# V's weights in load order, gates on ScalarE's queue, a fourth raw buffer, and mixed chunks in a layer with a product-key expert sub-layer

## The chip, the cores and the metric

One core of one Trainium2 chip. The time is in device microseconds (us) for one execution of the whole program; lower is better.

## The reference

One layer: adaptive norms, a mixing sub-layer (pooling and differential attention, projections in and out), a gated residual, then a sub-layer of 16384 single-neuron experts chosen by product keys, another gated residual and a final norm. The part that matters here, for 512 latent tokens of width 2048:

```
q = h @ Wq                        # 8 heads x 2 halves of 128
s1, s2 = q_half @ keys            # 128 scores for each half
top 16 of each half, then the top 16 of the 16 x 16 sums; g = softmax of them
expert e = 128 * i1 + i2
y = sum over heads and picks of  g * gelu(h . U[e]) * V[e]
```

## The kernel before

The program is one stream of work, dealt to five in-order engines by a scheduler that fixes each engine's order at build time. The stages of interest, in us of the profiled execution: norms and transposes to about 1153, queries ("wq", 16 half-heads, L626) to 1350, the first 72 tiles of U (L745) to 2053, then U's other 56 tiles and all of V to 3600, and the end.

For the last 368 latent tokens the experts are computed densely: for each of 128 blocks of 128 experts, a "u tile" makes gelu(h . U) by 48 matmuls (two loads of 512 KB from `ut`), is multiplied by a matrix of gates (mostly zero) and split into `a_hi` and `a_lo`; then V's rows of the block are multiplied by it. For the other 144 tokens SLOTS of single rows of U and V are gathered by GpSimd (`row`, `f`, `acc` in the names), and VectorE makes a multiply-add of 128x2048 of each (L696, L708). `pump` spreads them over the u tiles and the V loads.

Every weight comes by `weights()`: SyncE issues a load of 512 KB into one of 3 `raw` buffers (L126), ScalarE casts it to `whi` (L119), VectorE makes the rest `wlo` (L120; a_hi and a_lo, and fq_hi and fq_lo, go over the same two lines), each with 3 buffers, and TensorE makes three matmuls for each pair of pieces: hi by hi, hi by lo, lo by hi. In V a load is two rows of 512 numbers for each of 128 partitions and gives 24 matmuls (L953).

The gates of the dense tokens are built beside the first 72 u tiles and stored to DRAM (`g_s`). As they are complete only at the end, those 72 tiles are stored unmultiplied to `sg_s` ("kept" below; "spilled" in the title of the change). The last stage goes over 16 chunks of CH = 8 blocks: first 7 chunks of the 56 "fresh" blocks, whose u tiles are made there, then 9 chunks of the 72 kept ones, which are read back. For each 4 blocks a tile of gates `gt` (736 KB) is loaded. The names `raw`, `sg` (3 buffers, for fresh and kept tiles alike), `gt` (2 buffers) and `a_hi`, `a_lo` (9 each) are pools' tiles: a load waits until the tile that had its buffer has been read.

```
for c in range(NC):
    for n, ib in enumerate(ibs):                   # 8 blocks
        if n % 4 == 0: gt = ...; load gt           # L931
        sg = u_tile(ib, ...) or load sg_s[ib]      # L745, or L936
        sg = sg * gt                               # L937, VectorE
        a_hi, a_lo = split(sg)
    for dq in range(4):                            # four quarters of the output's width
        for n in range(0, 8, 2): weights(V ...); 24 matmuls   # L953
        accT[...] += pv[i]                         # L964, VectorE, four of them
```

Before the wq stage two more large copies matter: `f_hi` and `f_lo` (2944 KB each, packets of 368 numbers) are copied out of `fq_hi` and `fq_lo` by SyncE (L582, L583), and `keys` (1024 KB) is loaded by ScalarE (L604).

Of the kernel before, what the change touches and what calls it, by code (L numbers as in the profile page):

```python
# [10 lines left out]
F32 = mybir.dt.float32  # L11
# [18 lines left out]
NKEY = 128  # L30
# [4 lines left out]
GB = 16  # L35
# [30 lines left out]
SPILL = 72  # L66
# [4 lines left out]
GEND = 2  # L71
GRATE = 1.25
SLOTS = 256 + 2 * GB
RATE = (SLOTS - (SPILL - PRE - GS) * GRATE) / (2 * NKEY - SPILL - 11)


def body(tc, xin, ctx, vecs, lamv, ada1, ada2, adab2, n2g, fing, win, poolw, wout, wq, keys,
         ut, u, v, rope, icnt, out):
    nc = tc.nc
    V, S, G, E = nc.vector, nc.scalar, nc.gpsimd, nc.tensor  # L80

    with ExitStack() as whole:
        def pool(stack, name, bufs=1, space=None, side=None):
            kw = {} if space is None else {"space": space}
            if side is not None:
                kw["side"] = side
            if space is not DRAM:
                kw["reuse_waits"] = "tile"
            return stack.enter_context(tc.tile_pool(name=name, bufs=bufs, **kw))
# [28 lines left out]
        def split(dst_hi, dst_lo, src):  # L118
            S.copy(dst_hi, src)  # L119
            V.tensor_sub(dst_lo, src, dst_hi.bitcast(F32))  # L120

        def weights(src, shape):
            raw = wp.tile(shape, F32, name="raw", bufs=3)
            hi = wp.tile(shape, F32R, name="whi", bufs=3)
            lo = wp.tile(shape, F32R, name="wlo", bufs=3)
            nc.sync.dma_start(raw, src)  # L126
            split(hi, lo, raw)
            return hi, lo
# [87 lines left out]
        for k in range(KT):  # L216
            for j, c0, bs in ((0, 260, slice(2, 6)), (1, 2, slice(0, 2))):
                n = bs.stop - bs.start
# [370 lines left out]


        ub = pool(whole, "ub")
        ustack = ExitStack()
        psU = pool(ustack, "psU", 1, PSUM)
        rtstack = ExitStack()
# [81 lines left out]


        acc0 = gp.tile([128, D], F32, name="acc0")
        vw = v.rearrange("(a b) d -> a b d", b=NKEY)

        rows = [gp.tile([128, D], F32, name=f"row{i}") for i in range(3)]

# [74 lines left out]
        with ExitStack() as st:  # L757
            gb = pool(st, "gb")
            ps = pool(st, "psG", 1, PSUM)
            picks = {}  # L760

            def pick(b):
                ia, ib = (gb.tile([128, 128], F32, name=n, bufs=1) for n in ("ia", "ib"))
                gt = gb.tile([128, 128], F32, name="gt", bufs=1) if b else gate0
                decode(b, ia, ib, gt)
                if b == 0:
                    V.scalar_tensor_tensor(ia, ia, float(NKEY), ib, op0=OP.mult, op1=OP.add)
                    V.tensor_copy(e0, ia)
                    return
                if b == 1:  # L770
                    ef = gb.tile([128, 128], F32, name="ef")
                    ei = gb.tile([128, 128], I32, name="ei")
                    V.scalar_tensor_tensor(ef, ia, float(NKEY), ib, op0=OP.mult, op1=OP.add)
                    V.tensor_copy(ei, ef)
                    for q in range(GQ):
                        ps_, cs = slice(q * GB, (q + 1) * GB), slice(q * GB, (q + 1) * GB)
                        nc.scalar.dma_start(eB[ps_, :], ei[0:GB, cs])
                        nc.scalar.dma_start(gateB[ps_, :], gt[0:GB, cs])
                pt = ps.tile([128, 3, 128], F32, name="pt", bufs=1)
                for i, x in enumerate((ia, ib, gt)):  # L780
                    E.transpose(pt[:, i, :], x, ident)
                picks[b] = gb.tile([128, 3, 128], F32, name="pT", bufs=3)
                S.copy(picks[b], pt)

            def combine():

                for g in range(NG):
                    ge = gb.tile([128, 128, TG], F32, name="ge", bufs=1)
                    for t4 in range(0, TG, 4):
                        m = min(4, TG - t4)  # L790
                        pg = ps.tile([128, 4, 128], F32, name="pg", bufs=2)
                        for i in range(m):
                            b, t = divmod(T - TD + g * TG + t4 + i, 128)
                            pT = picks[b]
                            L = gb.tile([128, 128], F32, name="L", bufs=6)
                            R = gb.tile([128, 128], F32, name="R", bufs=6)
                            V.tensor_scalar(L, iota, pT[:, 0, t:t + 1], None, op0=OP.is_equal)
                            V.tensor_scalar(R, iota, pT[:, 1, t:t + 1], pT[:, 2, t:t + 1], op0=OP.is_equal, op1=OP.mult)
                            E.matmul(pg[:, i, :], L, R, start=True, stop=True)  # L799
                        S.copy(ge[:, :, t4:t4 + m].rearrange("p b t -> p t b"), pg[:, 0:m, :])  # L800
                        if t4 + 4 < TG:
                            yield
                    nc.scalar.dma_start(g_s[g], ge)
                    yield

            def few_end_steps():

                sel = gb.tile([128, GB], F32, name="sel")
                V.tensor_copy(sel, ident[:, 0:GB])
                for q in range(1, GQ):  # L810
                    V.tensor_add(sel, sel, ident[:, q * GB:(q + 1) * GB])
                z = gb.tile([128, D], F32, name="zB")[0:GB, :]
                ss = gb.tile([128, 4], F32, name="ssB")[0:GB, :]
                rs = gb.tile([128, 1], F32, name="rsB")[0:GB, :]
                tmp = gb.tile([128, 1], F32, name="tmpB")[0:GB, :]
                for dq in range(4):
                    ds = slice(dq * 512, (dq + 1) * 512)
                    gx = gb.tile([128, 512], F32, name="gxB", bufs=2)[0:GB, :]
                    nc.scalar.dma_start(gx, m_s[:, 3 * D + dq * 512:3 * D + (dq + 1) * 512].to_broadcast([GB, 512]))
                    xc = gb.tile([128, 512], F32, name="xcB", bufs=2)[0:GB, :]  # L820
                    nc.scalar.dma_start(xc, x1_s[1][0:GB, ds])
                    pb = ps.tile([128, 512], F32, name="pt", bufs=1)[0:GB, :]
                    E.matmul(pb, sel, acc0[:, ds], start=True, stop=True)
                    V.tensor_mul(z[:, ds], pb, gx)
                    V.tensor_add(z[:, ds], z[:, ds], xc)
                    S.activation(gx, z[:, ds], AF.Square, accum_out=ss[:, dq:dq + 1])
                    yield 1
                V.reduce_sum(rs, ss, axis=AX.X)
                V.tensor_scalar(tmp, rs, 1.0 / D, EPS, op0=OP.mult, op1=OP.add)
                G.tensor_tensor(rs, tmp, nhalf[0:GB, 0:1], OP.pow)  # L830
                for dq in range(4):
                    ds = slice(dq * 512, (dq + 1) * 512)
                    fg = gb.tile([128, 512], F32, name="gxB", bufs=2)[0:GB, :]
                    nc.scalar.dma_start(fg, fing[:, ds].to_broadcast([GB, 512]))
                    V.scalar_tensor_tensor(z[:, ds], z[:, ds], rs, fg, op0=OP.mult, op1=OP.mult)
                    nc.scalar.dma_start(out[128:128 + GB, ds], z[:, ds])
                    yield 1

            few_end_of.append(few_end_steps)
            spill(PRE)  # L840
            pick(1)
            steps = combine()
            todo, made, late = SPILL - PRE, 0, dict(LATE)
            nsteps = NG * ((TG + 3) // 4)
            for n in range(todo):
                spill(1)
                if n in late:
                    pick(late[n])
                if n >= GS:
                    pump(GRATE)  # L850
                while made < nsteps * (n + 1) / (todo - GEND):
                    made += 1
                    next(steps, None)
            assert made >= nsteps
# [40 lines left out]
        with ExitStack() as st:  # L895
# [23 lines left out]
                    if dq < 3:  # L919
                        V.tensor_mul(z[b][0:n, ds], z[b][0:n, ds], fg[0:n, :])  # L920

            order = list(range(SPILL, NKEY)) + list(range(SPILL))
            NC = NKEY // CH
            for c in range(NC):
                ibs = order[c * CH:(c + 1) * CH]
# [2 lines left out]
                for n, ib in enumerate(ibs):  # L928
                    if n % 4 == 0:
                        gt = ab.tile([128, NG, 4 * TG], F32, name="gt", bufs=2)  # L930
                        nc.sync.dma_start(gt, g_s[:, :, ib:ib + 4, :].rearrange("a p b t -> p a (b t)"))  # L931
                    if ib >= SPILL:
                        sg = u_tile(ib, bank()[:, 0:TD])
                    else:
# [9 lines left out]
                for dq in range(4):  # L944
                    pv = [bank()[:, 0:TD] for _ in range(4)]
                    for n in range(0, CH, 2):
                        hi, lo = weights(vw[:, ibs[n]:ibs[n] + 2, dq * 512:(dq + 1) * 512], [128, 2, 512])
                        for j in range(2):
                            a_hi, a_lo = A[n + j]
                            for i in range(4):  # L950
# [42 lines left out]
def prep(x, c, ctx, c_ctx, ada_w, ada_b, norm1_g, w_in, pool_w, pool_b, pool_scale,  # L993
         diff_lambda, subln_g, w_out, norm2_g, peer_wq, peer_keys, peer_u, peer_v, final_g):
    A = {}
# [24 lines left out]
    A["ut"] = peer_u[0].reshape(128, 128, 16, 128).transpose(1, 3, 2, 0)  # L1020
    A["u"] = peer_u[0]
    A["v"] = peer_v[0]
    f = np.float32
    t = np.arange(512)
    inv = (f(10000.0) ** (-np.arange(16, dtype=f) / f(16))).astype(f)
# [22 lines left out]
```

## Time and profile before

| what | us |
|---|---|
| median of 3 runs (lowest, highest) | 3621.0 (3616.66, 3635.32) |
| the profiled execution | 3616.92 |
| its span in the trace | 3615.1 |
| TensorE matmuls (PE) busy | 3473.2 (96%) |
| VectorE (DVE) busy | 2714.1 (75%) |
| ScalarE (ACT) busy | 1382.8 (38%) |
| GpSimd (POOL) busy | 525.6 (15%) |

A row of a timeline gives the start and the duration of an instruction (xN: of N merged ones), its line and its tiles as out<-in, and in brackets how long its engine sat idle before it and what ended that. SPq and ACTq are the queues of SyncE and ScalarE in which DMAs are issued. PEclk is TensorE's granted clock as a share of 2.4 GHz.

### The profile page before, as it was taken

What the parts mean: (1) busy time and instruction counts of PE and PEld (TensorE: products, weight loads), DVE (VectorE), ACT (ScalarE), POOL (GpSimd) and SP (SyncE); (2) the same over time, 40 slices, a digit from 0 to 9 for tenths busy, and PEclk for the clock granted to TensorE, in tenths of its full rate; (3) what the DMA queues carried; (4) which work ended last, traced back from release to release, by engine and by line L of the source; (5) the groups of instructions that cost most, each with busy time, mean ns of one, the idle gap of its engine ahead of it and who ended that gap; (6) DMA issues with size and microseconds to landing.
All of it is one profiled execution on the core that took longest, in us unless ns stands there. A gap on an engine that the chain in (4) does not pass through costs nothing.

```text
span 3615.1 us, 52998 instructions
## 1 busy us (share of the span) xinstructions
PE 3473.2 (96%) x20499; PEld 3230.3 (89%) x20499; DVE 2714.1 (75%) x4450; ACT 1382.8 (38%) x1987; POOL 525.6 (15%) x423
## 2 busy tenths in 40 slices
PE   7999999999998999999999999999999999999998
PEld 2588888899886889998999999999999999999998
DVE  5787787755536999997778677677677778888775
ACT  7554545555323223443334333223223322233233
POOL 1000000000031001111111122122122122112100
PEclk9999999999999999999999999999999999999999
DMA  9755555522547325887888887787787888988975
GB/s 332 266 178 173 173 170 176 156 66 72 197 140 217 112 91 207 307 292 285 289 315 325 295 324 267 277 325 266 282 327 287 287 321 313 322 317 316 318 242 173
DMA packets 295399, 885.74 MB, mean 245 GB/s; under 512 B 27345, under 2 KB 83386, under 8 KB 255466
## 3 DMA queue, kind: packets, MB, share of 16 engines
q1 hardware_dynamic: 223354, 494.45, 40.7%
q0 software_dynamic: 45600, 316.73, 22.9%
q10 hardware_dynamic: 26192, 71.18, 5.9%
q8 instruction: 160, 2.62, 0.3%
q14 instruction: 93, 0.76, 0.1%
HBM read 819.09 MB, written 51.35 MB: 241 GB/s over the span
## 4 chain that ended last, share of the span: by engine, by line
PE 57%; issue 14%; DMA 12%; DVE 10%; POOL 4%; ACT 4%; ACTq 0%; SPq 0%; DVEq 0%; POOLq 0%
PE pv L953 15%; PE pu L745 11%; PE zl L275 6%; PE pv L745 5%; PE pq L626 5%; PE zc L275 4%; PE pw L547 4%; DMA aw<-in_ada_dram 4%; DMA raw<-in_v_dram 3%; POOL row L690 2%; DVE wlo L120 2%; PE pg L799 2%; DMA sg<-sg_s 2%; DMA g_s<-ge 2%; PE sc L363 1%
## 5 line engine op out<-in xcount | busy, mean ns | idle before, releaser
L119 ACT CAST whi<-raw 128x1024 fp32r<-128x1024 f32 x664 | 695.5, 1050 | 1439.2 <-PE pv L953 305.9
L120 DVE TENSOR_TENSOR wlo<-raw,whi 128x1024 fp32r<-128x1024 f32 x664 | 822.7, 1244 | 429.6 <-ACT whi L119 420.4
L953 PE MATMUL pv<-a_hi,wlo 128*128 128x368 f32 x2048 | 684.0, 334 | 27.0 <-DVE wlo L120 27.0
L953 PE MATMUL pv<-a_hi,whi 128*128 128x368 f32 x2048 | 681.7, 333 | 8.1 <-ACT whi L119 8.1
L953 PE MATMUL pv<-a_lo,whi 128*128 128x368 f32 x2048 | 681.0, 333 | 0.0
L953 PEld LDWEIGHTS pv<-a_hi,wlo 128*128 128x128 f32 x2048 | 389.0, 190 | 32.8 <-DVE wlo L120 32.8
L953 PEld LDWEIGHTS pv<-a_hi,whi 128*128 128x128 f32 x2048 | 388.8, 190 | 9.5 <-ACT whi L119 9.5
L745 PE MATMUL pu<-f_hi,whi 128*128 128x368 f32 x1152 | 389.8, 338 | 1.3 <-ACT whi L119 1.0
L953 PEld LDWEIGHTS pv<-a_lo,whi 128*128 128x128 f32 x2048 | 388.7, 190 | 0.0
L745 PE MATMUL pu<-f_hi,wlo 128*128 128x368 f32 x1152 | 383.8, 333 | 4.0 <-DVE wlo L120 4.0
L745 PE MATMUL pu<-f_lo,whi 128*128 128x368 f32 x1152 | 381.1, 331 | 0.0
L745 PE MATMUL pv<-f_hi,whi 128*128 128x368 f32 x896 | 296.1, 330 | 1.3 <-ACT whi L119 1.3
L745 PE MATMUL pv<-f_hi,wlo 128*128 128x368 f32 x896 | 295.9, 330 | 1.2 <-DVE wlo L120 1.2
L745 PE MATMUL pv<-f_lo,whi 128*128 128x368 f32 x896 | 293.9, 328 | 0.0
L708 DVE SCALAR_TENSOR_TENSOR acc<-row,w,acc 128x2048 f32<-128x2048 f32 x111 | 260.6, 2347 | 0.0
L696 DVE SCALAR_TENSOR_TENSOR row<-row,f 128x2048 f32<-128x2048 f32 x109 | 248.6, 2287 | 9.6 <-DMA row<-in_u_dram,e 9.6
L275 PE MATMUL zl<-h_hi,whi 128*128 128x512 f32 (+1 forms) x640 | 239.2, 374 | 0.0
L690 POOL DMA_INDIRECT row<-in_v_dram,e x96 | 154.7, 1612 | 529.8 <-DVE acc L708 496.5
L275 PE MATMUL zl<-h_lo,whi 128*128 128x512 f32 (+1 forms) x640 | 223.7, 349 | 0.0
L275 PE MATMUL zl<-h_hi,wlo 128*128 128x512 f32 (+1 forms) x640 | 223.6, 349 | 0.0
L745 PEld LDWEIGHTS pu<-f_hi,wlo 128*128 128x128 f32 x1152 | 218.8, 190 | 4.9 <-DVE wlo L120 4.9
L745 PEld LDWEIGHTS pu<-f_hi,whi 128*128 128x128 f32 x1152 | 219.0, 190 | 2.8 <-ACT whi L119 1.9
(275 smaller groups left out, 6524.7 us busy)
## 6 DMA issues: line engine op xcount, KB each, us to landing
raw<-in_ut_dram SPq DMA_DIRECT2D x256, 512.0 KB
raw<-in_v_dram SPq DMA_DIRECT2D x256, 512.0 KB
aw<-in_ada_dram SPq DMA_DIRECT2D x256, 256.0 KB
raw<-in_win_dram SPq DMA_DIRECT2D x80, 512.0 KB
aw<-in_ada_dram SPq DMA_DIRECT2D x64, 512.0 KB
g_s<-ge ACTq DMA_DIRECT2D x8, 2944.0 KB
gt<-g_s SPq DMA_DIRECT2D x32, 736.0 KB
raw<-in_wout_dram SPq DMA_DIRECT2D x40, 512.0 KB
```

Source lines behind the costliest of these rows:

```text
L119: S.copy(dst_hi, src)
L120: V.tensor_sub(dst_lo, src, dst_hi.bitcast(F32))
L275: E.matmul(part[0], x[:, k8, :], y[:, k, part[1]], start=k == 0 and p == 0, stop=k == KT - 1 and p == 2)
L363: E.matmul(sc[:, cs], x[:, m, qs], y[:, cs], start=p == 0, stop=p == 1)
L547: E.matmul(pw[b], x[:, k, bs], y[:, j, :], start=i + j == 0 and p == 0, stop=i + j == KT - 1 and p == 2)
L626: E.matmul(pq[:, cs], a[:, k8, :], b[:, k, cs], start=k == 0 and p == 0, stop=k == KT - 1 and p == 2)
L690: G.indirect_dma_start(out=row, out_offset=None, in_=table, in_offset=bass.IndirectOffsetOnAxis(ap=e[:, j:j + 1], axis=0))
L696: tc.keep_in_program_order(V.scalar_tensor_tensor(row, row, 1.0, f0, op0=OP.mult, op1=OP.mult, accum_out=s0[:, j:j + 1]))
L708: tc.keep_in_program_order(V.scalar_tensor_tensor(acc0, row, w0[:, j:j + 1], acc0, op0=OP.mult, op1=OP.add))
L745: E.matmul(pu, a[:, k8, :], b[:, k, :], start=k == 0 and p == 0, stop=k == KT - 1 and p == 2)
L799: E.matmul(pg[:, i, :], L, R, start=True, stop=True)
L953: E.matmul(pv[i], x[:, j, ks], y, start=n + j == 0 and p == 0, stop=n + j == CH - 1 and p == 2)
```

## The change

Four edits. V's weights are handed over as a second copy `vd` in which the 4096 bytes that a partition takes in one load lie together (before: two pieces of 2048). The gates `gt` are issued from ScalarE's queue. Every fourth load goes into a further buffer `raw_0` that lies in the pool `ub`, from the wq stage on; its place is won by one buffer instead of two for `gxB` and `xcB`. And 14 chunks are made of 4 fresh and 4 kept blocks each, followed by 2 chunks of kept ones.

```
+RAWS = 1
+        turn, more = [0], []
+        def raw_buffer(shape):
+            turn[0] = (turn[0] + 1) % (3 + len(more))
+            if turn[0] < 3:
+                return wp.tile(shape, F32, name="raw", bufs=3)
+            return more[turn[0] - 3](shape)
         def weights(src, shape):
-            raw = wp.tile(shape, F32, name="raw", bufs=3)
+            raw = raw_buffer(shape)
...
         ub = pool(whole, "ub")
+        more.extend([lambda shape, i=i: ub.tile(shape, F32, name=f"raw_{i}") for i in range(RAWS)])
...
-                    gx = gb.tile([128, 512], F32, name="gxB", bufs=2)[0:GB, :]
+                    gx = gb.tile([128, 512], F32, name="gxB", bufs=1)[0:GB, :]
...
-            order = list(range(SPILL, NKEY)) + list(range(SPILL))
+            fresh, kept = list(range(SPILL, NKEY)), list(range(SPILL))
+            order = []
+            while fresh:
+                order += fresh[:4] + kept[:4]
+                fresh, kept = fresh[4:], kept[4:]
+            order += kept
...
-                        nc.sync.dma_start(gt, g_s[:, :, ib:ib + 4, :].rearrange("a p b t -> p a (b t)"))
+                        nc.scalar.dma_start(gt, g_s[:, :, ib:ib + 4, :].rearrange("a p b t -> p a (b t)"))
...
-                        hi, lo = weights(vw[:, ibs[n]:ibs[n] + 2, dq * 512:(dq + 1) * 512], [128, 2, 512])
+                        hi, lo = weights(vd[ibs[n] // 2, dq], [128, 2, 512])
...
+    A["vd"] = peer_v[0].reshape(128, 64, 2, 4, 512).transpose(1, 3, 0, 2, 4)
```

What this does to the engines' orders, at three places. **SyncE, start of the wq stage.** The names with `wq` are the loads of the half-heads, two for each; 11020 is the first load of the second half-head. Before:

```order
L126 DMA raw_11020<-in_wq_dram 128x1024
L126 DMA raw_11050<-in_wq_dram 128x1024
L126 DMA raw_11146<-in_wq_dram 128x1024
L126 DMA raw_11176<-in_wq_dram 128x1024
L582 DMA f_hi_10685<-fq_hi_10690 128x16x368
L583 DMA f_lo_10686<-fq_lo_10691 128x16x368
L126 DMA raw_11240<-in_wq_dram 128x1024
```

After:

```order
L136 DMA raw_11050<-in_wq_dram 128x1024
L136 DMA raw_11146<-in_wq_dram 128x1024
L136 DMA raw_11176<-in_wq_dram 128x1024
L592 DMA f_hi_10685<-fq_hi_10690 128x16x368
L593 DMA f_lo_10686<-fq_lo_10691 128x16x368
L136 DMA raw_0_11020<-in_wq_dram 128x1024
L136 DMA raw_0_11240<-in_wq_dram 128x1024
```

The load of 11020 now has the buffer `raw_0`, and stands behind the copies of f_hi and f_lo instead of ahead of the loads 11050 to 11176. It waits for the last of the tiles that lay in that place (the residual's rows, which the transposes and the copies of f to f0 read).

**SyncE, the passage from the u tiles to the V loads of a chunk.** Before, in the fifth of the fresh chunks, from the first load of V on:

```order
L126 DMA raw_24760<-in_v_dram 128x2x512
L126 DMA raw_24790<-in_v_dram 128x2x512
L126 DMA raw_24822<-in_v_dram 128x2x512
L126 DMA raw_24854<-in_v_dram 128x2x512
L126 DMA raw_24892<-in_v_dram 128x2x512
L126 DMA raw_24924<-in_v_dram 128x2x512
L931 DMA gt_25570<-g_s_79 128x8x184
L126 DMA raw_24954<-in_v_dram 128x2x512
```

After, in the seventh chunk, from the third load of V on (`sg` are the loads of the four kept tiles, called A4 to A7 below; the fresh ones are A0 to A3, and the loads of V v0 to v15, of which this row is v2):

```order
L136 DMA raw_0_25244<-in_vd_dram 128x1024
L136 DMA raw_25274<-in_vd_dram 128x1024
L136 DMA raw_25314<-in_vd_dram 128x1024
L136 DMA raw_25346<-in_vd_dram 128x1024
L952 DMA sg_25150<-sg_s_78 128x368
L952 DMA sg_25157<-sg_s_78 128x368
L136 DMA raw_0_25376<-in_vd_dram 128x1024
L952 DMA sg_25164<-sg_s_78 128x368
L952 DMA sg_25171<-sg_s_78 128x368
```

The gates have left this queue. Four loads of kept tiles stand between those of V: A4 and A5 behind v5, A6 and A7 behind v6.

**VectorE, the same passage.** Before, in the fifth chunk, from wlo of v3 on:

```order
L120 TENSOR_TENSOR wlo_24856<-raw_24854,whi_24855 128x1024
L708 SCALAR_TENSOR_TENSOR acc0_12695<-row2_12698,w0_13343,acc0_12695 128x2048
L120 TENSOR_TENSOR wlo_24894<-raw_24892,whi_24893 128x1024
L708 SCALAR_TENSOR_TENSOR acc0_12695<-f0_9445,w0_13343,acc0_12695 128x2048
L120 TENSOR_TENSOR wlo_24926<-raw_24924,whi_24925 128x1024
L708 SCALAR_TENSOR_TENSOR acc0_12695<-row0_12696,w0_13343,acc0_12695 128x2048
L964 TENSOR_TENSOR accT_19774<-accT_19774,pv_24756 128x368
L964 TENSOR_TENSOR accT_19774<-accT_19774,pv_24757 128x368
L964 TENSOR_TENSOR accT_19774<-accT_19774,pv_24758 128x368
L964 TENSOR_TENSOR accT_19774<-accT_19774,pv_24759 128x368
L120 TENSOR_TENSOR wlo_24956<-raw_24954,whi_24955 128x1024
```

After, in the seventh chunk, from the third gathered row behind the last u tile on:

```order
L718 SCALAR_TENSOR_TENSOR acc0_12695<-f0_9445,w0_13343,acc0_12695 128x2048
L121 TENSOR_TENSOR a_lo_25161<-sg_25157,a_hi_25160 128x368
L121 TENSOR_TENSOR a_lo_25168<-sg_25164,a_hi_25167 128x368
L953 TENSOR_TENSOR sg_25171<-sg_25171,gt_25148 128x368
L121 TENSOR_TENSOR wlo_25276<-raw_25274,whi_25275 128x1024
L121 TENSOR_TENSOR a_lo_25175<-sg_25171,a_hi_25174 128x368
L718 SCALAR_TENSOR_TENSOR acc0_12695<-row0_12696,w0_13343,acc0_12695 128x2048
L980 TENSOR_TENSOR accT_19774<-accT_19774,pv_25178 128x368
L980 TENSOR_TENSOR accT_19774<-accT_19774,pv_25179 128x368
L980 TENSOR_TENSOR accT_19774<-accT_19774,pv_25180 128x368
L980 TENSOR_TENSOR accT_19774<-accT_19774,pv_25181 128x368
L121 TENSOR_TENSOR wlo_25316<-raw_25314,whi_25315 128x1024
```

Before, wlo of v4 and v5 stood ahead of the four additions to accT that end the first quarter; now wlo of v4 stands behind them, and wlo of v3 behind the product of the last kept tile. Ahead of these rows stand, from the last u tile on, wlo of v2, product and a_lo of A3, a gathered row, the product of A4, a second gathered row, a_lo of A4 and the products of A5 and A6.

## Rows read from the trace of the kernel before

**Rows 1.** busy time of each engine in u and in V:
```profile
1350.00:2053.00 703.00, 679.48 (x4217) 669.08 (x4216) 597.99 (x1209) 281.50 (x335) 106.30 (x86) 0.99 0.79 289
2053.00:2936.00 883.00, 869.75 (x5143) 865.82 (x5141) 639.07 (x635) 273.26 (x328) 205.56 (x128) 0.99 0.81 296
2936.00:3600.00 664.00, 639.51 (x3744) 634.67 (x3744) 519.38 (x565) 209.13 (x267) 111.07 (x76) 0.98 0.83 289
```

**Rows 2.** busy time of TensorE's matmuls into pv, one undisturbed stretch:
```profile
2700.00:2900.00 200.00, 200.00 (x1197) 1.00 0.80 286
```

**Rows 3.** waits of TensorE, 2053 to 3600: us in total, times, longest:
```profile
PE pv L953 <- DVE wlo L120: 27.0, 18, 4.4
PE pv L953 <- ACT whi L119: 8.1, 4, 3.8
```

**Rows 4.** TensorE in the first and last of seven half-clock stretches:
```profile
2144.70:2147.90 3.20, 3.04 (x10) 0.50 0.50 111
...
3397.40:3400.60 3.20, 3.20 (x12) 0.50 1.02 335
```

**Rows 5.** SyncE in order of time: start, us, instruction:
```profile
2654.66 0.48 SPq L931 DMA_DIRECT2D gt<-g_s  x1
```

**Rows 6.** the chain that ended last, 2655 to 2680: start, us, what:
```profile
2659.17 16.68 DMA raw<-in_v_dram
```

**Rows 7.** SyncE in order of time at a kept chunk's start:
```profile
3042.08 1.29 SPq L936 DMA_DIRECT2D sg<-sg_s  x3
...
3050.08 3.01 SPq L936 DMA_DIRECT2D sg<-sg_s  x3
```

**Rows 8.** VectorE in order of time, the same place, idle time in brackets:
```profile
3043.76 2.35 DVE L708 SCALAR_TENSOR_TENSOR acc<-f,w,acc 128x2048 f32<-128x2048 f32 x1
3048.12 1.48 DVE L937 TENSOR_TENSOR sg<-sg,gt 128x368 f32<-128x368 f32 x3 [2.01 <-DMA sg<-sg_s]
...
3050.42 1.87 DVE L964 TENSOR_TENSOR accT<-accT,pv 128x368 f32<-128x368 f32 x4
...
3055.86 0.54 DVE L937 TENSOR_TENSOR sg<-sg,gt 128x368 f32<-128x368 f32 x1 [3.12 <-DMA sg<-sg_s]
```

**Rows 9.** DMA queues in 2300 to 2400: packets, MB, share of 16 engines:
```profile
q1 hardware_dynamic: 6545, 14.36, 41.8%
q0 software_dynamic: 1873, 13.65, 35.3%
```

**Rows 10.** SyncE in order of time at the start of the wq stage:
```profile
1154.97 5.91 SPq L583 DMA_DIRECT2D f_lo<-fq_lo  x1
1165.35 17.00 SPq L126 DMA_DIRECT2D raw<-in_wq_dram  x3
```

**Rows 11.** TensorE in order of time, the same place:
```profile
1165.77 0.40 PE L626 MATMUL pq<-fq_hi,whi 128*128 128x512 f32 x1
...
1170.58 0.39 PE L626 MATMUL pq<-fq_hi,whi 128*128 128x512 f32 x1
1174.51 1.39 PE L631 MATMUL pk<-keys,qT 128*128 128x128 f32 x8 [3.54 <-DMA keys<-in_keys_dram]
```

**Rows 12.** DMA share and GB/s (last two numbers) there:
```profile
1181.00:1183.00 2.00, 2.00 (x10) 1.67 (x9) 1.57 (x4) 0.00 (x0) 0.00 (x0) 1.00 0.48 187
```

**Rows 13.** ScalarE in order of time there:
```profile
1184.24 0.57 ACT L628 COPY qT<-pq 128x512 f32<-128x512 f32 x1
```

**Rows 14.** page, the costliest groups: busy, mean ns, idle before:
```profile
L119 ACT CAST whi<-raw 128x1024 fp32r<-128x1024 f32 x664 | 695.5, 1050 | 1439.2 <-PE pv L953 305.9
L120 DVE TENSOR_TENSOR wlo<-raw,whi 128x1024 fp32r<-128x1024 f32 x664 | 822.7, 1244 | 429.6 <-ACT whi L119 420.4
```

**Rows 15.** tile sg: duration ns min/median/max, first and last start:
```profile
L937 DVE TENSOR_TENSOR sg<-sg,gt x128: 533/537/546, 2070.8 to 3536.2; 128x368 f32<-128x368 f32 x128
L119 ACT CAST a_hi<-sg x128: 482/500/507, 2071.4 to 3537.5; 128x368 fp32r<-128x368 f32 x128
L120 DVE TENSOR_TENSOR a_lo<-sg,a_hi x128: 533/541/546, 2071.9 to 3538.0; 128x368 fp32r<-128x368 f32 x128
```

More of the change, by code (lines that the diff above doesn't have):

```diff
@@ L73 @@
 SLOTS = 256 + 2 * GB
+RAWS = 1
 RATE = (SLOTS - (SPILL - PRE - GS) * GRATE) / (2 * NKEY - SPILL - 11)
 def body(tc, xin, ctx, vecs, lamv, ada1, ada2, adab2, n2g, fing, win, poolw, wout, wq, keys,
-         ut, u, v, rope, icnt, out):
+         ut, u, v, vd, rope, icnt, out):
     nc = tc.nc
@@ L678, in body @@
         acc0 = gp.tile([128, D], F32, name="acc0")
-        vw = v.rearrange("(a b) d -> a b d", b=NKEY)
         rows = [gp.tile([128, D], F32, name=f"row{i}") for i in range(3)]
@@ L817, in few_end_steps @@
                     ds = slice(dq * 512, (dq + 1) * 512)
-                    gx = gb.tile([128, 512], F32, name="gxB", bufs=2)[0:GB, :]
+                    gx = gb.tile([128, 512], F32, name="gxB", bufs=1)[0:GB, :]
                     nc.scalar.dma_start(gx, m_s[:, 3 * D + dq * 512:3 * D + (dq + 1) * 512].to_broadcast([GB, 512]))
-                    xc = gb.tile([128, 512], F32, name="xcB", bufs=2)[0:GB, :]
+                    xc = gb.tile([128, 512], F32, name="xcB", bufs=1)[0:GB, :]
                     nc.scalar.dma_start(xc, x1_s[1][0:GB, ds])
@@ L832, in few_end_steps @@
                     ds = slice(dq * 512, (dq + 1) * 512)
-                    fg = gb.tile([128, 512], F32, name="gxB", bufs=2)[0:GB, :]
+                    fg = gb.tile([128, 512], F32, name="gxB", bufs=1)[0:GB, :]
                     nc.scalar.dma_start(fg, fing[:, ds].to_broadcast([GB, 512]))
```

## The prediction

> **What bounds the kernel now.** I read the busy times by stage first, then TensorE's waits, then the chain and the queues at the places of those waits. In V, TensorE is busy for 869.75 of 883 us and 639.51 of 664 [rows 1]; no other engine is near that. In an undisturbed stretch 1197 matmuls take 200 us, 0.167 us each [rows 2]. By that pace the 5143 + 3744 matmuls of the two stretches [rows 1] are worth 857.4 + 624.1 us, so V loses 25.6 us in its first part (fresh chunks) and 39.9 in the second (kept ones): **65.5 us**, all that an edit to loads and order can win there. The reader should see where it goes: the waits for wlo and whi are 35.1 us [rows 3], and they come in a few pieces of up to 4.4 us. Behind the longer ones the granted clock is 0.50, the level of 1.2 GHz, for 3.2 us or twice that [rows 4]; of the seven such stretches five have 3.2 us and two 6.4, 28.8 us in all, which cost half, 14.4 us. The remaining 16 us have no name in the waits; some matmul records may be missing too.
>
> Two mechanisms stand behind the waits. In a fresh chunk a gates load is issued at 2654.66 [rows 5], and the V load issued behind it at 2659.17 lands only after 16.68 us [rows 6], later than three buffers cover. In a kept chunk SyncE issues kept tiles at 3042.08 and 3050.08 [rows 7]; VectorE, which works in order, sits idle for them until 3048.12 and 3055.86, though other work (four accT, then a wlo) is queued behind [rows 8]. So a kept tile takes about 5.7 us from issue to use, and TensorE waits for the wlo behind it.
>
> **The layout of V, the queue of the gates and the fourth buffer** all work on the first mechanism. On q1 (SyncE's) 6545 packets took 41.8% of 16 x 100 us, 102 ns each; a gathered packet (q0) took 302 ns [rows 9]. A V load has 256 packets of 2048 bytes, 16 on each of 16 DMA engines. If one of each kind takes turns, that is 16 x 0.40 = 6.5 us when the gather is busy. With 128 packets of 4096 bytes, each bounded by twice 102 ns, it is 8 x 0.51 = 4.0 us. That shortens a load, and is worth something only where a load is late. With the gates on the other queue, the load of [rows 6] no longer stands behind 736 KB, and a fourth buffer lets SyncE run one load further ahead. I take it that all late V loads of the first mechanism vanish: -25.6 us for the fresh part, at the other bound nothing.
>
> The Trainium skill ("DMA: Bandwidth & Descriptors", section "Issuing engines are not separate DMA queues") says that transfers issued by different engines run on the same 16 DMA engines and interleave, so a second issuer saves issue time alone. The trace has one gates load on SyncE's queue ahead of the late load [rows 5, 6] and none on ScalarE's, so it can't say; by the rule alone the late loads would stay, which is the fourth rival below.
>
> ScalarE issues 32 gates loads more, at the 0.48 us of [rows 5]: 15 us on an engine busy for 273 of 883 us [rows 1], hidden by its idle time; uncovered, each would delay one cast by 0.5 us. Single gxB and xcB make few_end's eight steps wait for their own loads while the u stage keeps VectorE busy for 598 of 703 us [rows 1]. Each step could wait one landing, which the 5.7 us of the kept tiles stand for, but the next ones are slack for the u tiles: 0, with up to +5 as bound.
>
> **The fourth buffer at the start of the wq stage.** Its first user is the first load of the second half-head. In the order it has gone from ahead of f_hi and f_lo to behind them. SyncE is through with issuing f_lo at 1154.97 + 5.91 = 1160.9 [rows 10]. The two copies and keys then keep the DMA engines at work; from 1181 to 1183 their share is 0.48 [rows 12], which I read as full until about 1182. The load that was issued next before, at 1165.35 [rows 10], stood at the same place in the queue. So the load lands at about 1182, its cast takes 1.05 us [rows 14], and TensorE begins the half-head at about 1183. Before, it began at 1165.77, made 22 matmuls at 0.229 us until 1170.8, waited 3.54 us for keys [rows 11], and was through at 1184.24, when qT was read [rows 13]. After: 1183 + 48 x 0.229 = 1194.0, and about 2 us more for half clock behind so long an idle stretch (half of 3.2 to 6.4 us): 1196. That is **+12 us** (bounds: +0 if the load lands by 1170, +15 with a landing at 1183.3 and 6.4 us at half clock). What follows on TensorE has no idle time to give it back.
>
> **The mixed chunks.** The kept tiles of a chunk come now while TensorE goes from the 4th u tile (its end is T below) to V, 14 times. TensorE needs v0 and v1 with A0 to A3 from T, v2 with A4 and A5 from T+8, v3 with A6 and A7 from T+12 (24 matmuls of 0.167 us are 4 us), and v4 from T+16. I go through the order shown for the seventh chunk, with 1.05 us for a cast and 1.24 for a wlo [rows 14], 0.54, 0.50 and 0.54 for product, a_hi and a_lo [rows 15], 2.35 for a gathered row and 1.87 + 0.2 for four accT [rows 8], 0.43 us for an issue [rows 7].
> - whi of v2 gets its buffer at T, wlo of v2 ends at T+2.3, a_lo of A3 at T+3.95, the gathered row at 6.3.
> - SyncE waits with v5 for wlo of v1 (T-0.5), so A4 and A5 are issued from about T and land at T+5.7. Product of A4 6.85, gathered row 9.2, a_lo of A4 9.75. TensorE wants it at 8.2: 1.6 us lost.
> - Product of A5 10.3, of A6 (issued when A3's buffer is free, T+4, landed by 9.7) 10.85, gathered row 13.2, a_lo of A5 13.75; TensorE wants it at 11.8: 2.0 us lost.
> - A7 has A4's buffer, so it is issued at 9.75 and lands at 15.45. Product 16.0, wlo of v3 17.2; wanted at 15.9: 1.3 us lost. a_lo of A7 17.75, gathered row 20.1.
> - Four accT until 22.2, wlo of v4 23.4; wanted at 21.2: 2.2 us lost.
>
> Together 7.1 us. With kept tiles that land at once it would still be about 5.4: from T+1.05 on VectorE has three wlo (3.7), five products and a_lo (5.4), four gathered rows (9.4) and four accT (2.1) ahead of or as wlo of v4, 20.6 us, and v4 is wanted at T+16.3. The same walk through the orders of the second to fifth chunk gives 3.9, 5.7, 3.6 and 2.7 us for a landing of 4.7 us, and 5.5, 9.2, 7.2 and 4.7 for 6.3 (my bounds around the 5.7 of [rows 7, 8]); the seventh gives 6.2 and 7.8. Means 4.4 and 6.9; I take the middle, **5.6 us**, since 5.7 lies between the two landings. For the clock [rows 4] I add 1.0 us a chunk (0 to 2: a stretch of 3.2 us costs 1.6). 14 x 6.6 = 92 us. The two chunks of kept tiles alone, and the turn of the result, keep the second part's price of 39.9 us over 664, 8 us for the last 130 us.
>
> **Sum.** V loses 92 + 8 = 100 us in place of 65.5: +35. With wq +47. On the profiled execution's 3616.9 (its span is 3615.1, and the median of the runs 4 us above it): **3664 us**, say 3662. Written for any loss c in a mixed chunk: 3571.4 + 14c.
>
> **The rivals.** Some 0.5%, 18 us, is what a measurement here can tell from no change.
> - *The loads win* (0.21): the longer packets and the free queue let SyncE reach the kept tiles while u tiles still run, and VectorE has its products done before T. For it: VectorE is busy for 639 of 883 us [rows 1], so there is room on average. Against: three sg buffers, A6 and A7 can't be issued before A3 and A4 are done. It decides below c = 2.0; c = 1.5 gives 3592, faster.
> - *It cancels* (0.22): c between 2.0 and 4.5, as in the fourth and fifth chunks at the short landing. c = 3.3 gives 3618.
> - *The forecast* (0.47): c between 4.5 and 8.9, 3634 to 3696.
> - *The gates collide all the same* (0.10): V loads go on being late by the first part's 25.6 us over 7 chunks, 3.7 us in each of the 14, on top: c = 10.3, 3716.
> - *The wq load isn't late* would take 12 us off any of these; I hold it for unlikely, since the order shows it behind 5.9 MB.
>
> The range leaves half of the first rival below 3592 and most of the last above 3702. Faster by over 0.5% 0.21, within 0.5% 0.22, slower 0.57.
>
> The Trainium skill (the same page, section "Queues, rings and completion order") states that a DMA engine takes turns between its queues packet by packet. The numbers of [rows 9] fit that, but don't show it; it is what would make longer packets a larger share, the ground of the first rival.
>
> **What would show it.** Right: the first matmul of the second half-head only at about 1183, the u stage begun some 12 us later; in V 14 passages with several short waits for wlo whose releasers, followed back, are kept tiles or products on VectorE, no V load that lands after over 10 us, and more half-clock stretches than seven. Wrong: passages with one wait of a microsecond or none, or kept tiles issued well before T; or V loads still late behind the gates. A span of V below 1535 us (2053 to 3600 before) would refute the term of the mixed chunks; a u stage begun where it was would refute the wq term.

## The result, and the profile after

The changed kernel takes 3677.5 us (3676.3 to 3681.0), 1.0153 times the time of before (95% interval 1.013 to 1.0175): slower, 15 us above the forecast and inside its range. The profiled execution has a span of 3676.2 us, 61.1 more than before.

Where the 61 us came from is read off the first and last starts of the matmuls that read f_hi (duration ns min/median/max, first and last start):

```profile
L755 PE MATMUL pu<-f_hi,whi x1152: 325/331/606, 1365.2 to 2064.2; 128*128 128x368 f32 x192
...
L755 PE MATMUL pv<-f_hi,whi x896: 325/330/439, 2065.0 to 3453.7; 128*128 128x368 f32 x180
```

The matmuls of the u tiles that are stored begin 14.6 us later (before at 1350.6), their stage is 3.5 us shorter, and V, from the first matmul of its own u tiles to the last addition to accT, lasts 1595.1 us instead of 1544.7: +50.4.

At the start of the wq stage, TensorE in order of time:

```profile
1171.54 2.05 PE L642 MATMUL pk<-keys,qT 128*128 128x128 f32 x8 [5.79 <-DMA keys<-in_keys_dram]
1184.01 0.79 PE L637 MATMUL pq<-fq_hi,whi 128*128 128x512 f32 x1 [10.42 <-ACT whi L120]
```

and the chain that ended last there (start, us, what):

```profile
1166.86 16.03 DMA raw<-in_wq_dram
...
1182.91 2.95 ACT whi L120 x3
```

The first load of the second half-head is issued only at 1166.86 and lands at 1182.9; TensorE begins that half-head at 1184.0, after 10.42 us idle. Before it had begun at 1165.77 [rows 11].

In V, TensorE's waits (us in total, times, longest), to hold against [rows 3]:

```profile
PE pv L969 <- DVE a_lo L121: 32.8, 17, 7.3
PE pv L969 <- DVE wlo L121: 16.9, 9, 2.3
PE pv L969 <- ACT a_hi L120: 16.8, 7, 7.1
PE pv L969 <- ACT whi L120: 6.1, 8, 2.6
```

35.1 us of waits for V's weights were there before; now 23.0 for those, and 49.6 for a_lo and a_hi, the halves of the expert tiles, which do not appear in [rows 3]. The half-clock stretches (before: seven, 28.8 us, [rows 4]) are twelve with 72.5 us in all; the longest three:

```profile
2318.90:2332.40 13.50, 6.18 (x20) 0.50 0.54 201
2530.50:2540.50 10.00, 7.35 (x22) 0.50 0.78 267
2636.30:2646.30 10.00, 7.57 (x24) 0.50 0.62 229
```

They are longer than the 3.2 or 6.4 us of before, and TensorE is busy for only 6 of 13.5 us in the first: further waits lie inside them.

What the layout, the queue and the buffer were to do has happened. ScalarE's casts in V, with the idle time ahead of them and what ended it:

```profile
L120 ACT CAST whi<-raw 128x1024 fp32r<-128x1024 f32 x343 | 360.0, 1050 | 817.7 <-PE pv L969 552.8 <-PE pv L755 222.2 <-DMA raw<-in_vd_dram 16.3
```

The loads of V end 16.3 us of its idle time; in the same window of the kernel before it was

```profile
L119 ACT CAST whi<-raw 128x1024 fp32r<-128x1024 f32 x356 | 373.7, 1050 | 812.6 <-PE pv L953 286.6 <-DMA raw<-in_v_dram 273.3 <-PE pv L745 196.8
```

that is, 273.3 us.

### The profile page after: what moved, and what is told of

Its sections match the earlier page's. It is cut to its first block, busy times and chain, and to the rows that moved or that the text cites. A ratio compares the mean times of both kernels' runs of the same rounds, so it can differ in the third digit from the quotient of the medians.

```text
span 3676.2 us, 52992 instructions
## 1 busy us (share of the span) xinstructions
PE 3489.8 (95%) x20499; PEld 3240.6 (88%) x20499; DVE 2718.2 (74%) x4450; ACT 1387.6 (38%) x1989; POOL 497.0 (14%) x423
## 4 chain that ended last, share of the span: by engine, by line
PE 73%; DMA 11%; DVE 10%; ACT 3%; issue 2%; POOL 1%; ACTq 0%; SPq 0%; DVEq 0%; POOLq 0%
PE pv L969 24%; PE pu L755 13%; PE pv L755 11%; PE zl L285 6%; PE pq L637 5%; PE zc L285 4%; DMA sg<-sg_s 4%; PE pw L557 4%; DMA aw<-in_ada_dram 3%; PE pg L809 2%; DVE wlo L121 2%; DMA g_s<-ge 2%; PE sc L373 1%; DVE aacc L442 1%; PE o L404 1%
## 5 line engine op out<-in xcount | busy, mean ns | idle before, releaser
L969 PE MATMUL pv<-a_lo,whi 128*128 128x368 f32 x2048 | 688.6, 337 | 32.8 <-DVE a_lo L121 32.8
L969 PE MATMUL pv<-a_hi,wlo 128*128 128x368 f32 x2048 | 673.7, 335 | 16.9 <-DVE wlo L121 16.9
L755 PEld LDWEIGHTS pu<-f_lo,whi 128*128 128x128 f32 x1152 | 218.9, 190 | 0.0
```

Source lines behind the costliest of these rows:

```text
L755: E.matmul(pu, a[:, k8, :], b[:, k, :], start=k == 0 and p == 0, stop=k == KT - 1 and p == 2)
L969: E.matmul(pv[i], x[:, j, ks], y, start=n + j == 0 and p == 0, stop=n + j == CH - 1 and p == 2)
```

## The experiments

Each run was timed beside the kernel before on the same chip. V is measured as above; "waits" are all of TensorE's in it.

| run | median us | ratio to before (95%) | V, us | waits in V, us |
|---|---|---|---|---|
| the kernel before | 3617 to 3624 | 1 | 1544.7 | 37.6 |
| the changed kernel | 3677.5 | 1.0153 (1.013 to 1.0175) | 1595.1 | 72.6 |
| x1_unmixed | 3583.8 | 0.9891 (0.9853 to 0.993) | 1504.4 | 12.4 |
| x2_raw0_from_u | 3667.0 | 1.011 (1.0071 to 1.0149) | 1605.6 | 81.3 |
| x3_kept_first | 3595.1 | 0.9925 (0.990 to 0.995) | 1511.2 | 17.8 |
| x9_kept_first_raw0_from_u | 3584.7 | 0.989 (0.9854 to 0.9927) | 1511.7 | 17.0 |
| x5_own_kept_buffers | 3654.4 | 1.0096 (1.0069 to 1.0123) | 1567.3 | 54.7 |
| x8_unmixed_raw0_from_u | 3569.5 | 0.9863 (0.9841 to 0.9885) | 1502.7 | 10.5 |
| p_layout | 3582.8 | 0.9899 (0.988 to 0.9918) | 1510.8 | 16.9 |
| p_gates | 3601.0 | 0.9953 (0.9935 to 0.9971) | 1530.6 | 30.9 |
| p_fourth_buffer | 3580.0 | 0.9903 (0.988 to 0.9927) | 1513.5 | 18.1 |
| p_layout_gates | 3576.0 | 0.9891 (0.9871 to 0.9911) | 1509.7 | 13.9 |
| p_mixed | 3700.9 | 1.0239 (1.0214 to 1.0264) | 1626.2 | 90.3 |
| x10_unmixed_six_kept_buffers | 3566.8 | 0.9869 (0.9847 to 0.9892) | 1501.1 | 9.2 |

**x1_unmixed.** The old order of chunks in the changed kernel.

```
-            while fresh:
-                order += fresh[:4] + kept[:4]
...
+            order = list(range(SPILL, NKEY)) + list(range(SPILL))
```

> The changed kernel with the old order of chunks (7 of fresh blocks, then 9 of kept ones); V's layout, the gates' queue and the fourth buffer stay. My theory: the mixed passages cost V about 86 us of its 116 us of losses. Without them the fresh part loses little, about 5 us instead of the 25.6 of the kernel before, the kept part its old 40, the wq stage stays 14 us late: about 3607. Rival (loads still late behind gates on another queue, whatever the order): V keeps 25 us in its fresh part, about 3630. Rival (the mix is not the cause): about 3675.

3583.8 us, 23 below my 3607: the mix alone cost 94 us, more than I gave it, and the other three edits are worth more than the fresh part's 25.6 us. V is 40 us shorter than before. TensorE's waits in V, and ScalarE's casts:

```profile
PE pv L964 <- DVE wlo L121: 12.4, 9, 2.6
```

```profile
L120 ACT CAST whi<-raw 128x1024 fp32r<-128x1024 f32 x366 | 384.1, 1050 | 780.9 <-PE pv L964 545.5 <-PE pv L755 201.6 <-issue 8.6
```

The landing of a V load no longer stands among the causes of idle time, in the chunks of kept tiles neither. The rival with loads late behind the gates falls.

**x3_kept_first.** The same blocks in the same mixed chunks, the kept ones ahead.

```
-                order += fresh[:4] + kept[:4]
+                order += kept[:4] + fresh[:4]
```

> The changed kernel with the kept tiles as the first four of each mixed chunk and the fresh ones as the last four, so that kept tiles can be read, multiplied and split while TensorE makes the chunk before and the fresh u tiles. Same numbers of loads, products and gathers. My theory (kept tiles come last, on VectorE's in-order path between the last u tile and V): the waits for a_lo and a_hi vanish, 1 to 2 us left in a passage instead of 7.7: 3676 - 14 x 6 = 3590. Rival (a mixed chunk is dear by its traffic: u, V and kept tiles at once): as the changed kernel, 3665 to 3680.

3595.1 us, 82 less than the changed kernel, as my theory had it, and the rival of the dear traffic falls: every load, product and gathered row is still there. What makes the difference is shown by two rows of VectorE's waits, of the changed kernel and of this one:

```profile
DVE sg L953 <- DMA sg<-sg_s: 72.0, 33, 7.4
```

```profile
DVE sg L953 <- DMA sg<-sg_s: 63.5, 28, 9.1
```

VectorE sits idle for kept tiles nearly as long, 63.5 us. But TensorE waits for no a_lo and no a_hi any more:

```profile
PE pv L969 <- DVE wlo L121: 11.2, 12, 3.2
```

An idle VectorE costs only where what is queued behind the late tile is the next thing that TensorE wants.

**x5_own_kept_buffers.** Kept tiles still last in the chunk, with buffers of their own.

```
-                        sg = ub.tile([128, NG, TG], F32, name="sg", bufs=3)
+                        sg = ab.tile([128, NG, TG], F32, name="sk", bufs=3)
                         nc.sync.dma_start(sg..., sg_s[ib])
...
-        xc = fn.tile(..., name="xc", bufs=2)       and the same for by_column's
+        xc = fn.tile(..., name="xc", bufs=1)
```

> The changed kernel (fresh tiles first, as it stands) with three buffers of their own for the kept tiles; the room is taken from two small pools of the end (one buffer instead of two). In the order the kept tiles A4 to A6 are now read a whole chunk ahead, only A7 is read in the passage, but a_lo of A4 to A7, wlo of v3 and v4 and the gathered rows stay in nearly the old order on VectorE. My theory (VectorE's work in that order, not the landing, makes most of a passage's loss): one to two us less of the 7.7 in a passage: 3650 to 3662. Rival (the kept tiles' landing makes it): only A7 is left, 2 us in a passage: 3595 to 3610.

3654.4 us, within what my theory gave, but the run does not part VectorE's work from the landing as it was meant to. TensorE's waits:

```profile
PE pv L969 <- DVE wlo L121: 33.6, 17, 4.6
PE pv L969 <- ACT a_hi L120: 11.0, 5, 3.1
...
PE pv L969 <- DVE a_lo L121: 3.6, 7, 1.7
```

The waits for a_lo fall from 32.8 to 3.6 us, those for wlo double from 16.9: A4 to A6 are there, but V's weights are still behind A7 and the gathered rows in VectorE's order. And VectorE goes on waiting for DMAs:

```profile
DVE sk L953 <- DMA sk<-sg_s: 43.5, 17, 6.1
DVE sk L953 <- DMA gt<-g_s: 42.6, 5, 13.6
```

A7 has A4's buffer and is issued only behind a_lo of A4, so its landing is still in the passage (43.5 us of idle time for kept tiles, 72.0 in the changed kernel). The tiles that are multiplied earlier now wait for their gates (42.6 us, 4.1 in the changed kernel). By the 28 us that V is shorter, taking the landing of A4 to A6 out gives back 2 of the 7.7 us that a passage loses, net of these gates. How much of the rest is A7's landing and how much VectorE's work in that order stays open: x3 took both out of the passage at once.

**x2_raw0_from_u.** The list of further buffers is filled only after the wq stage.

```
-        more.extend([lambda shape, i=i: ub.tile(...) for i in range(RAWS)])
         ustack = ExitStack()
...
         qstack.close()
+        more.extend([lambda shape, i=i: ub.tile(...) for i in range(RAWS)])
```

> The changed kernel, but the fourth buffer is first used by the loads of U, so that all loads of the wq stage have the three old buffers. My theory: the second half-head begins before the copies of f_hi and f_lo again, the u stage begins 14 us earlier, nothing downstream changes: 3676 - 14 = 3662. Rival (the idle time only moves to the next stage, since VectorE has its sorting to do): within 4 us of the changed kernel.

The stored u tiles begin at 1348.5 again (tile f_hi: duration ns min/median/max, first and last start):

```profile
L755 PE MATMUL pu<-f_hi,whi x1152: 325/331/512, 1348.5 to 2046.4; 128*128 128x368 f32 x192
```

So the 14.6 us belong to that load. The total fell only by 10 us, to 3667.0, between my forecast and the rival's, as V took 10.5 more. The fourth buffer falls on other loads in this version (the turn is counted from another start), and so the order in the passages isn't the same; whether that makes those 10 us was not tried. With the kept tiles ahead the same edit gave 10 us by the medians too, with a V that is the same to 0.5 us:

**x9_kept_first_raw0_from_u.** Both edits.

> The two edits of the other runs together: kept tiles first in the mixed chunks, fourth buffer only from the loads of U on. If the two costs are independent the gains add: 3676 - 84 - 14 = 3578, faster than both kernels. If the idle time of the wq stage or of the passages is only moved, it ends above 3600.

3584.7 us, 1.1% faster than the kernel before. That is 7 above what I expected, but by the parts as measured (82.4 with the kept tiles first, 10.5 with the buffer from U on) the sum is 3584.6: the two gains add.

**x8_unmixed_raw0_from_u.** The changed kernel without its two dear parts, by the edits of x1 and x2.

> Old order of chunks and the fourth buffer from the loads of U on; V's layout and the gates' queue as in the changed kernel. The wq stage should give back 14 us of the 3584 measured with the old order: 3568 to 3574, 1.4% faster than the kernel before. If the idle time moves on, 3580.

3569.5 us, 1.4% faster than before: 14.3 less than x1.

**p_layout, p_gates, p_fourth_buffer, p_layout_gates, p_mixed.** The parts in the kernel before. Each is the hunk of the change for that part; the fourth buffer is used from the loads of U on.

```
p_layout:         weights(vd[ibs[n] // 2, dq], [128, 2, 512])
p_gates:          nc.scalar.dma_start(gt, ...)
p_fourth_buffer:  raw_buffer(shape) in weights(), gxB and xcB with bufs=1
p_mixed:          order += fresh[:4] + kept[:4]
```

> The kernel before with V's new layout alone. V loses 65 us there; with the layout, the gates' queue and the fourth buffer together 25. If packets of 2048 against the gather's long ones make the loads late, this part alone wins 20 to 30 us, 3590 to 3600. If it is the gates ahead of the loads, or the number of buffers, under 8 us.

> The kernel before with the gates on ScalarE's queue alone. By my prediction the late loads of the fresh part (25 us) go with the gates: 3590 to 3600. By the rule that all queues share the DMA engines, nothing moves: 3615 to 3625.

> The kernel before with the fourth buffer alone, from the loads of U on. If late loads are a matter of how far SyncE may run ahead, one load more (4 us of TensorE's work) takes most of the late landings: 3590 to 3600. If the loads behind a gates tile or a kept tile stay behind it, 3610 to 3620.

> The kernel before with V's layout and the gates' queue, three buffers, old order of chunks. Alone they gave 3583 and 3601 against 3620 (37 and 18 us of the 65 that V loses). If they cure the same late loads, both together are near 3580; if they add, 3565, and the fourth buffer gives nothing to the 3570 that all three give.

3582.8, 3601.0, 3580.0 and 3576.0 us. The layout alone and the buffer alone win 37 us each, the gates 18, layout and gates together 41, all three (x8) 50: they don't add. The layout and the buffer give more than either of their forecasts; the gates end just above mine and below the one by the rule. ScalarE's idle time that the landing of a V load ended, 273.3 us before, is to be read in these three rows, of p_layout, p_gates and p_fourth_buffer:

```profile
L119 ACT CAST whi<-raw 128x1024 fp32r<-128x1024 f32 x365 | 383.3, 1051 | 802.3 <-PE pv L952 356.2 <-DMA raw<-in_vd_dram 198.2 <-PE pv L744 190.3
```

```profile
L119 ACT CAST whi<-raw 128x1024 fp32r<-128x1024 f32 x361 | 379.3, 1051 | 796.5 <-DMA raw<-in_v_dram 306.7 <-PE pv L953 231.5 <-PE pv L745 189.2
```

```profile
L120 ACT CAST whi<-raw 128x1024 fp32r<-128x1024 f32 x362 | 379.8, 1050 | 784.6 <-PE pv L964 479.3 <-PE pv L755 204.1 <-DMA raw<-in_v_dram 72.2
```

With the gates moved, ScalarE waits more for V's loads than before, 306.7 us, and in the fresh part a V load still lands late (chain, start, us):

```profile
2652.25 13.28 DMA raw<-in_v_dram
```

It is the next load in the order, issued 10 us after a gates tile on the other queue, where the one of 16.68 us was issued 4.5 us after one on its own [rows 5, 6]; so at this place a load is late with the gates on either queue. The fourth buffer does most for the casts. The layout and the buffer thus both relieve the late loads; by what the gates' queue gains, these rows don't show.

> The kernel before with the mixed chunks alone. In the changed kernel the mixed order cost 92 us (3676 against 3584). If that cost is VectorE's order in the passage and not the loads, it comes on top here too, with late loads beside it: 3690 to 3730. If the other edits made the mix dear (gates on ScalarE's queue, long packets ahead of the kept tiles), it costs less here: below 3660.

3700.9 us, 84 more than the kernel before. The mix costs about as much without the other three edits as with them (94), and the waits are of the same kinds:

```profile
PE pv L958 <- DVE a_lo L120: 34.1, 22, 4.4
PE pv L958 <- ACT a_hi L119: 29.3, 13, 10.9
PE pv L958 <- DVE wlo L120: 19.5, 14, 2.6
```

So neither the long packets nor the gates on ScalarE's queue nor the fourth buffer made the mix dear.

**x10_unmixed_six_kept_buffers.** x8 with two sets of three buffers for the kept tiles.

> The fastest version so far (old order of chunks, fourth buffer from the loads of U on, new layout, gates on ScalarE's queue) with six buffers for the kept tiles instead of three. What is left there are 7 waits for wlo, 10.5 us, five of the seven in the chunks of kept tiles. If kept tiles' landing is what VectorE sits idle for ahead of those wlo, 8 us less: 3562. If it is the order on VectorE alone, as in the run with own kept buffers, no change: 3566 to 3572.

3566.8 us (3564.9 to 3573.8) against 3569.5 (3564.4 to 3570.6): no difference that can be told. TensorE's waits for wlo there are 8.8 us instead of 10.5.

## Why the forecast was right

**The wq term** was +12 and measured 14.6. The load lands at 1182.9 (said 1182) and TensorE begins at 1184.0 (said 1183), so 1 us is the landing's. Behind the two waits the clock stays low until 1189, and the half-head makes its first nine matmuls at that clock (the whole stretch with all engines, then its end with TensorE alone):

```profile
1168.60:1189.00 20.40, 6.37 (x17) 4.76 (x18) 8.25 (x35) 3.52 (x4) 0.00 (x0) 0.50 0.74 259
...
1184.00:1189.00 5.00, 4.32 (x9) 0.50 0.51 161
```

Nine matmuls at 0.229 us are 2.1 us. They took 5.0, of which 0.67 is a wait for the second load's cast, so 2.9 us were lost where I had put 2 for the clock. The last 0.7 us has no name. One detail I had otherwise: the load is issued not behind f_lo at 1161 but at 1166.86, as SyncE waits 5.5 us until the copies of f to f0 on ScalarE's queue are through. It landed within 1 us of my time all the same; whether an earlier issue would have landed earlier was not tried.

**The mixed passages** were given as 6.6 us each, 5.6 in waits and 1.0 for the clock. Measured: V loses 65.5 + 50.4 = 116 us, less 8 for the last two chunks 108, 7.7 us each (those two took 67.3 and 68.4 us for 64 us of matmuls). The waits are 72.6 us, all but 2.3 of them in the passages, 5.0 each. The twelve half-clock stretches, 72.5 us long, hold 50.48 us of TensorE's work (the last line of their view):

```profile
sum 72.50, PE 50.48; mean PE 4.21
```

Half of that work, 25 us, is what the clock cost, 1.8 us a passage; the other 22 us of the stretches are idle time, which is in the waits already. So the clock's term was mis-sized by a factor of 1.8, just inside the bound of 2 us that I had set: I reckoned with one short stretch a passage, while several waits close together make stretches of 6.4 to 13.5 us. Waits and clock make 6.8 of the 7.7 us; 0.9 has no name.

That the mean of the waits fits is in part luck, for none of the five passages that I walked through lost what its walk gave. TensorE waited 8.6, 9.6, 3.1 and 6.8 us in those of the second to fifth chunk, where the two landings had given 3.9 to 5.5, 5.7 to 9.2, 3.6 to 7.2 and 2.7 to 4.7; in the seventh it was 2.8, where they gave 6.2 to 7.8. Nor are the waits those that I had named as a sign, for wlo (16.9 us); most are for a_lo and a_hi (49.6). VectorE in the passage worked out, the seventh, where T is 2730.6:

```profile
2737.01 0.54 DVE L953 TENSOR_TENSOR sg<-sg,gt 128x368 f32<-128x368 f32 x1 [0.20 <-DMA sg<-sg_s]
...
2739.73 0.54 DVE L121 TENSOR_TENSOR a_lo<-sg,a_hi 128x368 fp32r<-128x368 f32 x1
...
2743.35 0.99 DVE L121 TENSOR_TENSOR a_lo<-sg,a_hi 128x368 fp32r<-128x368 f32 x2
2744.32 0.54 DVE L953 TENSOR_TENSOR sg<-sg,gt 128x368 f32<-128x368 f32 x1
2744.78 1.22 DVE L121 TENSOR_TENSOR wlo<-raw,whi 128x1024 fp32r<-128x1024 f32 x1
...
2748.63 1.87 DVE L980 TENSOR_TENSOR accT<-accT,pv 128x368 f32<-128x368 f32 x4
2750.42 1.22 DVE L121 TENSOR_TENSOR wlo<-raw,whi 128x1024 fp32r<-128x1024 f32 x1
```

Product of A4 ends at T+6.9 (said 6.85), a_lo of A4 at 9.7 (9.75), a_lo of A5 and A6 at 13.7 (13.75 for A5). The product of A7 begins at 13.7 and not at 15.45, as its tile landed within 4 us and not in 5.7, and wlo of v4 ends at 21.0 (23.4). But TensorE lost there 2.8 us, not 7.1:

```profile
PE pv L969 <- DVE wlo L121: 2.1, 1, 2.1
PE pv L969 <- DVE a_lo L121: 0.4, 1, 0.4
PE pv L969 <- ACT whi L120: 0.3, 1, 0.3
```

Two steps failed. The first is "TensorE wants it at": I took the order of the matmuls from the code's loops, where each product of a_hi with whi is followed by one with a_lo. TensorE in order of time:

```profile
2738.72 0.83 PE L969 MATMUL pv<-a_hi,whi 128*128 128x368 f32 x4
2739.86 0.44 PE L969 MATMUL pv<-a_hi,whi 128*128 128x368 f32 x1 [0.30 <-ACT whi L120]
2740.13 0.62 PE L969 MATMUL pv<-a_lo,whi 128*128 128x368 f32 x2
```

The four products of a_hi of A4 with whi come in a row, then one that waits for the cast of v4, and only then the first with a_lo; so a late a_lo is partly covered. The second is the landing, which I had at 5.7 us (4.7 to 6.3). In the third chunk the loss is 9.6 us, 7.3 of it here:

```profile
PE pv L969 <- DVE a_lo L121: 7.3, 1, 7.3
```

```profile
2312.49 12.56 DMA sg<-sg_s
```

A6 took 12.56 us from issue to use, twice the 5.7 of [rows 7, 8]; VectorE stood still for 7.24 of them. Beside it the gather and a gates tile are under way (2312 to 2326: packets, MB, share of 16 engines):

```profile
q0 software_dynamic: 386, 2.77, 48.7%
q1 hardware_dynamic: 549, 1.05, 20.1%
q10 hardware_dynamic: 1040, 0.75, 16.7%
```

Packets of 736 bytes on q10 (ScalarE's queue, the gates) and the gathered rows on q0 share the engines with 549 on q1. That would be the mechanism of the fourth rival, at a kept tile rather than a V load. That the gates make the landing long was not isolated. It is not the choice of their queue, for in p_mixed, with the gates on SyncE's, VectorE stands still for 11.45 us for kept tiles in the second chunk, and TensorE waits 10.9 us behind them:

```profile
2220.30 1.02 DVE L942 TENSOR_TENSOR sg<-sg,gt 128x368 f32<-128x368 f32 x2 [11.45 <-DMA sg<-sg_s]
```

**The late V loads** should vanish, -25.6 us, in the fresh part alone. They did vanish, but the three edits are worth 40 us of V (x1), in the chunks of kept tiles too: there I had kept the old price. The second mechanism of the kernel before, the kept tile, was hence not the only one at work there. In this sum the old price stands for the last two chunks alone, and there the 8 us came out. So the +61 of the span are wq +14.6 (said 12), V +50.4 (said 35, and the difference lies in the passages) and the u stage -3.5 (said 0; it is between 695 and 708 us long in the runs, so that part tells nothing).

Two readings in the prediction are loose. 200 us for 1197 matmuls are 0.1671 us each, by which V lost 62 us and not 65.5 before; that is worth 3 us of the sum. And the 102 and 302 ns of [rows 9] are means that take in packets of 4 bytes and, on q1, of 736 and 4096; by size that stretch of the trace has 100 ns for 2048 bytes, 182 for 4096 and 338 for a gathered packet, which makes 7.0 and 4.2 us of the 6.5 and 4.0; the sum doesn't use them.

**The rule of the Trainium skill** on issuing engines ("DMA: Bandwidth & Descriptors", section "Issuing engines are not separate DMA queues") agrees with p_gates as far as the loads go: 306.7 us of ScalarE's idle time end with a V load there, 273.3 before. Still that kernel is 0.5% faster, 3601.0 us where the rule alone gave 3615 to 3625. In V of the kernel before, SyncE waited for a free gates buffer with V's loads behind:

```profile
SPq L931 <- DVE sg L937: 31.8, 14, 5.3
```

In p_gates SyncE has no such wait. Whether that is the gain was not isolated.

## What to carry to other kernels

A tile that another stage could have made long ago is dear when the loop makes it last, in front of the engine that sets the pace: look at what an in-order engine has between the last tile and the first thing the next stage wants, and put the tiles that only need reading ahead of those that must be computed. Three edits that shorten the same stage don't add (37, 18 and 37 us alone, 50 together), so time each of them alone before they are bundled with an edit of another kind; here the bundle hid 50 us of gain behind two costs. And the first user of a new buffer waits for whatever lay in its place: put that user where a load has slack.

## What the runs showed of the hardware that was not expected

Stretches at 1.2 GHz were 3.2 or 6.4 us long in the kernel before; with several waits close together they lasted 10 to 13.5 us in three passages, and 20.4 us at the start of the wq stage. In V the clock cost some 25 us, a third of the 72.6 us of the waits themselves. A read of 184 KB, 5.7 us before, took 12.56 us in one passage, with a gates tile and gathered rows under way; what made it long was not isolated.
